# A hybrid decoder layer: from whole-sequence stages in program order to eight interleaved 512-token tiles ordered by a build-time list scheduler

## The chip, the cores and the metric

The kernel runs on all eight cores of one Trainium2 chip. Each core computes two of the sixteen sequences; the cores do not exchange data. The metric is the device time of the slowest core, in microseconds (us). A core has a matrix engine (TensorE, PE in the profile; its weight loads are PEld), a vector engine (VectorE, DVE), a scalar engine (ScalarE, ACT), GpSimd (POOL) and SyncE (SP, which here only issues DMA). Each engine takes its instructions from its own list, in the order in which the program put them there.

The program has a fast and a slow state. In the slow state the cores of one die, or of both, show a lower granted clock and the run takes some per cent longer. Where a median is quoted, it is that of all runs of its kernel, slow ones included; ratios are of fast runs alone.

## The reference

One decoder layer, batch 16, sequence 2048, width 1024. Cut to what matters here:

```python
def swiglu(x, w_gate, w_up, w_down):                 # w: 1024x2816, 1024x2816, 2816x1024
    return (silu(x @ w_gate) * (x @ w_up)) @ w_down

mod = silu(c) @ w_ada + b_ada                        # nine vectors: shift, scale, gate for 3 sub-layers
u = modulate(rmsnorm(h, ffn1_norm), sh1, sc1)
h = h + 0.5 * g1 * swiglu(u, ...)                    # FFN1
u = modulate(rmsnorm(h, mix_norm), sh2, sc2)
h = h + g2 * hybrid_mixer(u, ...)                    # causal attention: 4 differential + 4 latent heads,
                                                     # rope by positions, combined in/out projections
u = modulate(rmsnorm(h, ffn2_norm), sh3, sc3)
h = h + 0.5 * g3 * swiglu(u, ...)                    # FFN2
return rmsnorm(h, final_norm)
```

## The kernel before

The hidden state of a whole sequence (128 x 8 x 2048 fp32) stays in SBUF, and the stages run one after another in program order, for sequence 0 and then for sequence 1. Activations are kept transposed: the width lies on the partitions, so the sum of squares over the width needs a matmul with a matrix of ones.

```python
for s in range(nseq):                                # two sequences per core
    if s > 0:
        load_x(s)
    norm_mod(0, s); ffn(0, s, plans[(s, 0)])         # hooks that spread the adaLN blocks: cut
    norm_mod(1, s); mixer(s, plans[(s, "mix")])
    norm_mod(2, s); ffn(2, s, plans[(s, 1)])
    final_store(s)
```

The norm statistics are squared on ScalarE or VectorE in bf16, and summed by eight matmuls with ones, one for each chunk of 128 of the width:

```python
def stats(srcs, split=True):
    pb = psall.next()                                # one rotation over all eight PSUM banks
    for k, (ap, res) in enumerate(srcs):
        sq, sqR = btmp.next()
        ...                                          # square on DVE or ACT
        I("pe", "matmul", r=[sqR, onesR], w=[PR[pb]], out=PS[pb][:], lhsT=ones_sb[:], rhs=sq[:],
          start=(k == 0), stop=(k == n - 1))
    return pb
```

Weights lie in HBM as fp32. Each use fetches a block through GpSimd's DMA queue, which casts to bf16 on the way, into one of five buffers. A block is used for all 2048 tokens of a sequence before it is released, so a core reads each FFN weight twice in all.

The softmax here doesn't subtract the row's maximum and nothing guards it: scores larger than these inputs give would overflow.

## Time and profile before

Three runs: 3640.93, 3645.35 and 4089.76 us, median 3645.35. The last is slow. (The result below counts a fourth run, 3662.38 us.) In the profiled run all cores lie between 3627.8 and 3640.0 us.

| | before |
|---|---|
| span of the slowest core | 3640.0 us |
| TensorE busy | 3025.7 us, 83% |
| VectorE, ScalarE, GpSimd busy | 50%, 33%, 3% |
| bytes moved by DMA, as counted | 143.53 MB |

The page of the profile, first lines, then three rows of its 40 slices (91 us each): the busy tenths of TensorE, the granted TensorE clock in tenths, and the busy tenths of the DMA engines. Last, a group of VectorE instructions: its line, engine, operation, operands, shape and count, then busy us and the mean ns of one, then the idle time before them.

```profile
span 3640.0 us, 42738 instructions; the slowest of 8 cores (3627.8 to 3640.0 us)
PE 3025.7 (83%) x16784; PEld 1435.4 (39%) x16784; DVE 1828.8 (50%) x3549; ACT 1194.5 (33%) x2001; POOL 98.3 (3%) x121
...
PE   1899996779777769999939999947887777799996
...
PEclk8899998889888879999959999978898887899998
DMA  9243343002001021221361222110010100222112
...
L125 DVE TENSOR_TENSOR ft<-hT,rs 128x512 f32<-128x512 f32 x192 | 117.7, 685 | 133.1 <-ACT rs L125 133.1
```

The nines are the feed-forward networks. The sevens and eights between them (slices 6 to 14 and 26 to 34, counted from 0) are the mixer and its norms. In the same slices the clock row shows mostly 8 and 7: where TensorE has gaps, the granted clock in the records is lower too.

The windows view gives stretches with numbers: the stretch, its length, then busy us (and count) of PE, PEld, DVE, ACT and POOL, the granted clock, the DMA share and GB/s. The four stretches are the start, a norm phase with what is around it, the second half of a mixer, and a feed-forward network.

```profile
0.00:91.00 91.00, 16.26 (x152) 6.04 (x152) 11.76 (x37) 25.23 (x41) 8.97 (x14) 0.85 1.01 184
560.00:700.00 140.00, 88.24 (x454) 37.04 (x453) 106.86 (x197) 65.44 (x109) 5.09 (x6) 0.80 0.21 30
910.00:1365.00 455.00, 328.05 (x2252) 175.44 (x2250) 261.56 (x589) 259.14 (x443) 5.03 (x6) 0.85 0.10 16
1365.00:1820.00 455.00, 452.08 (x2062) 200.07 (x2062) 191.10 (x281) 54.14 (x103) 15.02 (x18) 1.00 0.24 37
```

The last row is dense: 452 of 455 us busy, at clock 1.00. The timeline inside it shows ScalarE's evacuation of one gate bank after every 16 matmuls (eight gate, eight up). Its columns are start, duration, the instruction, and in brackets how long it had waited and for whom:

```profile
1379.59 0.60 ACT L125 ACTIVATE ft<-psall 128x512 f32<-128x512 f32 x1 [2.86 <-PE psall L125]
...
1383.04 0.60 ACT L125 ACTIVATE ft<-psall 128x512 f32<-128x512 f32 x1 [2.86 <-PE psall L125]
```

They come 3.45 us apart, so a matmul of 128x512 takes 3.45 / 16 = 215.6 ns. The Trainium skill, "TensorE: Matmul & The Clock Gate", section "Back-to-back issue gap", gives N / 2.4 + 2.5 ns as the gap of an isolated warm matmul of N columns, 215.8 ns for 512, and says that a sustained stream with weight loads needs only about 131 ns. This trace, a stream with one weight load for each matmul (2062 of each in the last row), agrees with the formula and not with the 131 ns. I use that form below as the **ideal** time of TensorE: each matmul of N columns counts N / 2.4 + 2.5 ns, but one of 129 columns 57 ns (in this trace eight took 0.63 us, and in long runs of them one takes 57 ns) and one of 2 columns 30 ns (a round figure; in this trace they mostly start 25 ns apart). The **lost** time of a stretch is its length less the ideal time of its matmuls. It holds idle time and time at a reduced clock together. For the kernel before, the ideal is 2742 us, and the lost time is 3640 - 2742 = about 900 us: 82 us in the first 91 us, and 334 and 333 us in the two mixers with their norms (560 to 1400 and 2370 to 3200); the rest is spread over norms and seams.

The waits view of TensorE (who was waited for, us in all, times, longest) names what it idles for:

```profile
PE psall L125 <- ACT bt L125: 302.3, 71, 31.0
PE psall L125 <- DVE obf L125: 72.1, 28, 8.5
```

`bt` holds the squares of the norms and the rope inputs, and `obf` is the attention output before its transpose. Neither engine is full; the stages only run one after another.

### The profile page before, as it was taken

How to read it: one execution, taken by the hardware profiler on the slowest of the kernel's cores; microseconds unless marked ns; L12 is line 12 of the kernel's file. 1: busy time of each engine (PE TensorE's matmuls, PEld its weight loads, DVE VectorE, ACT ScalarE, POOL GpSimd, SP SyncE). 2: the span in 40 equal slices, each digit the busy share in tenths (PEclk: the TensorE clock that was granted, in tenths of full speed). 3: DMA queues.
4: the chain of work that ended last, by engine and by line, in shares of the span. 5: the costliest groups of instructions: out<-in, count | busy, mean ns of one | idle time of the engine just before them, and what ended most of it. 6: DMA issues, size and time to landing. Idle time of an engine off the chain costs nothing.

```text
span 3640.0 us, 42738 instructions; the slowest of 8 cores (3627.8 to 3640.0 us)
## 1 busy us (share of the span) xinstructions
PE 3025.7 (83%) x16784; PEld 1435.4 (39%) x16784; DVE 1828.8 (50%) x3549; ACT 1194.5 (33%) x2001; POOL 98.3 (3%) x121
## 2 busy tenths in 40 slices
PE   1899996779777769999939999947887777799996
PEld 0344442344435424444314444424443254344442
DVE  1343447757574462344642334666766645433337
ACT  2301005363636651100152010065454564511112
POOL 0000000000000000000000000000000000000000
PEclk8899998889888879999959999978898887899998
DMA  9243343002001021221361222110010100222112
GB/s 184 44 79 59 58 64 50 15 1 29 1 14 20 13 35 24 42 46 24 52 194 24 35 47 30 24 21 10 15 15 4 29 13 1 35 47 45 26 18 93
DMA packets 123178, 143.53 MB, mean 39 GB/s; under 512 B 5984, under 2 KB 91232, under 8 KB 122976
## 3 DMA queue, kind: packets, MB, share of 16 engines
q0 software_dynamic: 100944, 102.83, 18.6%
q1 hardware_dynamic: 22032, 37.96, 3.6%
q8 instruction: 132, 2.16, 0.2%
q14 instruction: 70, 0.57, 0.1%
HBM read 226.82 MB, written 16.78 MB: 67 GB/s over the span
## 4 chain that ended last, share of the span: by engine, by line
PE 66%; DVE 17%; ACT 10%; issue 3%; DMA 2%; SPq 2%; ACTq 0%; DVEq 0%; POOLq 0%
PE psall L125 66%; DVE hT L125 5%; DVE ft L125 3%; ACT uT L125 3%; DVE accsb L125 3%; ACT ptbuf L125 2%; ACT bt L125 2%; ACT rs L125 2%; SPq L125 2%; DVE small L125 1%; DVE wb L125 1%; DVE bigA L125 1%; DMA hT<-xT 1%; DMA lam_sb<-lamv 1%; DVE junk L125 1%
## 5 line engine op out<-in xcount | busy, mean ns | idle before, releaser
L125 PE MATMUL psall<-uT,wb 128*128 128x512 bf16 (+2 forms) x6688 | 1520.2, 388 | 51.8 <-DVE ft L125 36.9
L125 PEld LDWEIGHTS psall<-uT,wb 128*128 128x128 bf16 (+2 forms) x6688 | 664.1, 100 | 881.0 <-issue 74.7
L125 DVE SCALAR_TENSOR_TENSOR hT<-psall,SC,hT 128x512 f32<-128x512 f32 x960 | 653.3, 744 | 134.1 <-PE psall L125 127.2
L125 ACT ACTIVATE ft<-psall 128x512 f32<-128x512 f32 x352 | 185.6, 601 | 1419.8 <-PE psall L125 1418.2
L125 ACT ACTIVATE ptbuf<-psall 128x512 bf16<-128x512 f32 (+2 forms) x608 | 419.4, 766 | 150.8 <-PE psall L125 146.0
L125 DVE TENSOR_TENSOR bigA<-ft,psall 128x512 bf16<-128x512 f32 x192 | 131.8, 687 | 501.8 <-PE psall L125 483.7
L125 PE MATMUL psall<-bigB,ptbuf 128*128 128x129 bf16 x3264 | 321.3, 233 | 53.4 <-ACT ptbuf L125 27.1
L125 PE MATMUL psall<-bt,ones_sb 128*128 128x512 bf16 x328 | 146.6, 513 | 235.9 <-ACT bt L125 223.5
L125 DVE TENSOR_TENSOR bigB<-ft,psall 128x512 bf16<-128x512 f32 x160 | 109.8, 686 | 455.9 <-PE psall L125 451.7
L125 PE MATMUL psall<-bigA,wb 128*128 128x512 bf16 x1536 | 333.5, 379 | 0.0
L125 PE MATMUL psall<-bigB,wb 128*128 128x512 bf16 x1280 | 292.9, 380 | 4.5
L125 PEld LDWEIGHTS psall<-bigB,ptbuf 128*128 128x128 bf16 x3264 | 223.2, 103 | 147.6 <-ACT ptbuf L125 81.8
L125 PE MATMUL psall<-bigA 64*128 64x512 bf16 (+3 forms) x1216 | 235.7, 334 | 21.8 <-DVE bigA L125 15.6
L125 ACT ACTIVATE bt<-hT 128x512 bf16<-128x512 f32 x256 | 138.3, 616 | 318.9 <-DVE hT L125 160.1
L125 PEld LDWEIGHTS psall<-bigA,wb 128*128 128x128 bf16 x1536 | 150.0, 98 | 180.5
L125 DVE COPY accsb<-psall 128x258 f32<-128x258 f32 x192 | 81.7, 426 | 212.1 <-PE psall L125 208.4
L125 PEld LDWEIGHTS psall<-bigB,wb 128*128 128x128 bf16 x1280 | 117.7, 98 | 176.8 <-DVE hT L125 47.3
L125 DVE TENSOR_TENSOR ft<-hT,rs 128x512 f32<-128x512 f32 x192 | 117.7, 685 | 133.1 <-ACT rs L125 133.1
L125 PEld LDWEIGHTS psall<-bt,ones_sb 128*128 128x128 bf16 x328 | 32.5, 102 | 347.4 <-ACT bt L125 168.5
L125 DVE TENSOR_TENSOR ft<-bigB,psall 128x512 f32<-128x512 bf16 (+1 forms) x208 | 136.5, 682 | 51.5 <-PE psall L125 43.5
L125 PE MATMUL psall<-wb 128*128 128x512 bf16 x512 | 128.2, 405 | 27.4 <-DVE wb L125 18.5
L125 ACT ACTIVATE uT<-ft,SC 128x512 bf16<-128x512 f32 x192 | 138.0, 800 | 19.5 <-DVE ft L125 19.5
(70 smaller groups left out, 1536.3 us busy)
## 6 DMA issues: line engine op xcount, KB each, us to landing
wb<-wg POOLq DMA_DIRECT2D x20, 1024.0 KB, 9.1
wb<-wu POOLq DMA_DIRECT2D x20, 1024.0 KB, 9.6
wb<-wd POOLq DMA_DIRECT2D x20, 1024.0 KB, 9.0
wb<-w_ada POOLq DMA_DIRECT2D x18, 1024.0 KB, 14.8
hT<-xT SPq DMA_DIRECT2D x64, 256.0 KB, 11.9
outT<-hT SPq DMA_DIRECT2D x64, 256.0 KB, 3.6
wb<-w_in POOLq DMA_DIRECT2D x12, 512.0 KB, 5.6
posi<-pos SPq DMA_DIRECT2D x16, 256.0 KB, 3.3
```

Source lines behind the costliest of these rows:

```text
L125: ins = getattr(eng, o.fn[0])(**o.fn[1])
```

## The change

The intent is to give TensorE other work while attention and norms leave gaps. The kernel is rewritten:

- The two sequences are cut into eight tiles of 512 tokens. While attention of tile t runs, FFN2 of tile t-1 and FFN1 of tile t+1 are interleaved with it. K and V of earlier tiles go to HBM and come back.
- Operations are recorded in a graph, each with a cost and a "virtual time" that spreads it over the segment in which it was recorded (`seg(a, b)`). At build time a list scheduler gives each engine, whenever that engine is free, the ready operation of the lowest virtual time. The list is then fixed; on the chip every engine follows it in order.
- Weights are now needed once per tile, not once per sequence. The first use loads fp32 through GpSimd's queue as before, and writes the bf16 block back to HBM; every later use reads the bf16 copy through SyncE's queue.
- The squares of a norm and their sum over the eight chunks move to GpSimd: eight products and seven additions, in a chain, 128x512 each; one matmul with ones is left. Silu is built from tanh.
- The eight PSUM banks are split: 0, 1, 2 rotate for the feed-forward networks (`fb`), 3, 4, 7 for the mixer (`mb`), and attention accumulates in 5 and 6.

The diff is a rewrite of nearly all lines; its core, with cuts marked:

```diff
+fb = Rot([0, 1, 2])                       # PSUM banks of the feed-forward networks, in turn
+mb = Rot([3, 4, 7])
-psall = Rot(list(range(8)))
...
+def load(self, src, scr, key, ...):       # class Ring: weight buffers
+    if key not in self.seen:              # first use: fp32 in, bf16 back to HBM
+        G.dma("pool", ..., out=buf, in_=src)
+        G.dma("sp", ..., out=scr, in_=buf)
+    else:                                 # later uses
+        G.dma("sp", ..., out=buf, in_=scr)
...
+def sumsq(srcs, bank, dim):
+    ...                                   # GpSimd: 8 products, 7 additions -> ar
+    MM(bank, PS[bank], onesf[:], ar[:], True, True, [arR, onesR])
+    ...                                   # ScalarE: Ln, Exp -> rs
...
+for t in range(NT):
+    s1 = 0 if t == 0 else 1
+    base = 2.0 * t if t else 1.0
+    ...                                   # norm for the mixer, spill of h
+    if not last:
+        with G.seg(base + 0.1, base + 0.4, eng="pool"):
+            load_x(t + 1, 1)
+            st1 = hstats(1, fb.next())    # norm statistics of tile t+1: takes a feed-forward bank
+    if t > 0:
+        with G.seg(base, base + 0.667, lead=0.05):
+            gate_up(1)                    # FFN2 of tile t-1: takes feed-forward banks in turn
+    if not last:
+        with G.seg(base + 0.667 if t else 0.9, base + 0.7 if t else 1.0):
+            apply_norm(1, 0, (t + 1) // 4, st1, uF, uFR, ntmp)
+    ...                                   # down(1), final(t-1), gate_up(0) of t+1, projections,
+                                          # attention, out_proj, norm for FFN2, down(0)
```

## The prediction

It was made before any run of the changed kernel, from the profile before, the two programs, and the order of the built program's instructions.

> **What bounds it now.** TensorE, but only in places. In a dense feed-forward stretch (timeline at 1380 us) 16 matmuls of 128x512 take 3.455 us, 215.9 ns each, at a granted clock of 1.00 (windows, 1365:1820). The program has 6.44 million matmul columns; at that rate they need 2714 us (estimate from 215.9 ns per 512). The span is 3640 us. The other 926 us: TensorE idle 614 us (busy 3026), and about 310 us of busy time at a reduced clock. Both sit in the start (0:91 us: TensorE busy 16 us, DMA saturated), the norm phases and the mixer: windows 560:700, 910:1365 and 2730:3185 show TensorE 63 to 74% busy and clock 0.80 to 0.85. The waits view names ACT's norm squares (302 us), rope, attention evacuation and exponentials. VectorE (50%) and ACT (33%) bind only locally: stages run one after another.
>
> **What the change does.** TensorE work hardly shrinks: the built program has 6.23 million columns (mask matmuls and most ones-matmuls gone; norm sums move to GpSimd), estimate 2640 us at 215.9 ns per 512 and 57 ns per 128x129 (eight took 0.63 us in the timeline). The gain is packing: feed-forward matmuls fill the gaps of attention (built order: 4 feed-forward matmuls, 12 PV, 3 QK, ...), so idle and low clock should both vanish in the middle.
> Other engines, counts of the built program times durations here: VectorE about 1450 us (352 gate products at 0.74, 352 up products at 0.69, 208 rope products at 0.68, ...), ACT about 1200 us (736 exponentials at 0.54 to 0.64, 352 tanh at 0.52 to 0.60) plus some 100 table switches at 1.28 us (31 before). Neither reaches 60%.
> Added: weights are reloaded for every 512 tokens from a bf16 copy in HBM, 290 MB, with 150 MB of other traffic and 122 MB of fp32 loads. Before, the first 91 us read about 300 GB/s with DMA full, so some 1.9 ms of DMA, hidden except where fp32 loads, write-back and reloads coincide.
>
> **Sum (estimates).** 2640 TensorE; +60 start before the first feed-forward matmul; +105 in tile 0, whose 34 weight blocks cost 5.2 us each (1 MB fp32 read, 0.5 MB written back) against 3.45 us of matmuls, plus adaLN weights; +20 for the same in the second feed-forward; +55 at the end (last norm, last feed-forward alone, 16 chained GpSimd operations, store); +100 of small waits (static order against true durations, table switches, three PSUM banks per side). Total 2980 us, 18% less. All of the gain lies on the critical path, since TensorE is that path.
>
> **Range and chances.** 2830 to 3190 us. Faster by over 2%: 0.95; within 2%: 0.03; slower: 0.02.
>
> **What the profile would show.** TensorE over 90% busy and clock at least 0.97 from slice 5 to 38; slices 1 to 4 thin, with DMA near full; the chain of waits mostly matmuls, then DMA at the start; ACT table loads near 100.
>
> **What would make it wrong.** (1) The clock. The Trainium skill, "TensorE: Matmul & The Clock Gate", Part 1, says that three or more cores of a die on dense matmuls fall to 13/16. This trace disagrees (1.00 with eight cores dense), but one of three runs took 4090 us, which 13/16 in the dense 1824 us would explain. If denser work brings that state on, about 3400 us. (2) GpSimd's additions and two-input VectorE operations share a port (skill, "SBUF — State Buffer", Who interferes with whom; not shown here): VectorE delays stall the banks. (3) Reload bandwidth when all cores stream. (4) Better packing than I grant: 2800.

Its "about 300 GB/s" is an estimate that counts what the casting loads read, fp32. The windows view counts the bf16 that they write, 184 GB/s; counted the other way, the trace has some 280 GB/s (8.6 MB from casting loads, taken twice, and 8.2 MB from others in 91 us).

## The result

| | before | after |
|---|---|---|
| median of the runs beside each other | 3653.86 us | 3206.95 us |
| all after runs | | 3202.4 to 3207.08 us |
| ratio of fast runs | 1 | 0.8782, 95% interval 0.8747 to 0.8816 |

A ratio here is the mean time of one kernel's fast runs over the mean time of the other's of the same rounds. It is therefore not quite the ratio of the medians quoted. (The median of before in these rounds is pulled up by a slow run.)

The change saves 12%, and the prediction had said 18%: 3207 us against 2980, and outside its range of 2830 to 3190.

The page after, in the same cut (a slice is now 80 us), with two of its VectorE groups, and its line on the chain of waits that ended last:

```profile
span 3204.9 us, 39963 instructions; the slowest of 8 cores (3189.3 to 3204.9 us)
PE 2779.3 (87%) x15704; PEld 1358.9 (42%) x15704; DVE 1382.9 (43%) x2800; ACT 1154.4 (36%) x1996; POOL 693.6 (22%) x670
...
PE   0646789688998999899998999899997999998988
...
PEclk9876789899999999999998999999999999998989
DMA  8999796797554464544435456644754464443123
...
PE 70%; DMA 10%; POOL 7%; DVE 7%; ACT 4%; issue 1%; SPq 1%; POOLq 0%; DVEq 0%; ACTq 0%
...
L303 DVE TENSOR_TENSOR actv<-ft,psall 128x512 bf16<-128x512 f32 x352 | 241.5, 686 | 206.4 <-PE psall L303 205.2
...
L303 DVE TENSOR_TENSOR nt<-h,rs 128x512 f32<-128x512 f32 x128 | 92.5, 743 | 182.2 <-ACT rs L303 174.4
```

The sevens and eights of the mixers are gone. Two things are new. The first ten slices are mostly thin, with DMA at 6 to 9 tenths. And the row of nines is broken by an eight (once a seven) every four or five slices, which is once per tile.

Windows: the start up to the statistics of the first norm, in which TensorE runs only 96 small adaLN matmuls (2 columns each) and one with ones; the rest of the start and tile 0 until just behind its first down-projection, whose last matmul ends at 319 us; the rest of tile 0; tile 1; and tile 3 as one of the steady tiles.

```profile
0.00:75.00 75.00, 3.14 (x97) 2.94 (x97) 2.76 (x18) 2.99 (x4) 29.39 (x37) 1.00 0.83 152
75.00:345.00 270.00, 153.62 (x755) 64.82 (x754) 119.05 (x224) 35.41 (x55) 60.85 (x75) 0.75 0.95 201
345.00:572.00 227.00, 211.70 (x1271) 105.00 (x1272) 120.53 (x285) 88.15 (x147) 60.27 (x70) 0.91 0.83 189
572.00:966.00 394.00, 333.51 (x1776) 159.69 (x1776) 166.34 (x326) 132.01 (x224) 93.62 (x96) 0.94 0.72 186
1333.00:1724.00 391.00, 368.16 (x2253) 189.85 (x2251) 163.19 (x325) 182.10 (x321) 78.08 (x68) 0.98 0.47 142
```

With the lost time computed as before (ideal 2652 us in all, so 553 us lost), set against the terms of the prediction's sum. I read its "+60" and "+105" as the start and tile 0, its "+20" as tile 1, and divide its "+100 of small waits" over what is left:

| stretch | lost, measured | predicted | difference |
|---|---|---|---|
| 0 to 572 us: start and tile 0 | 72 + 149 + 33 = 254 | 60 + 105 = 165 | +89 |
| 572 to 966: tile 1 (first use of the FFN2 weights) | 75 | 20 | +55 |
| 966 to 2775: tiles 2 to 6 | 152 | 100 | +52 |
| 2775 to 3205: last tile and end | 72 | 55 | +17 |
| sum | 553 | 340 | +213 |

Adding the differing ideal (2652 against 2640) gives 225 us, which is the distance from 2980 to the profiled 3205.

TensorE's waits after:

```profile
PE psall L303 <- POOL ar L303: 178.2, 28, 39.3
PE psall L303 <- DMA wf<-w_ada: 41.5, 5, 23.0
PE psall L303 <- DVE ft L303: 34.8, 14, 8.6
PE psall L303 <- DVE cab L303: 32.6, 1, 32.6
```

The first line is the new one. `ar` is the sum of squares that GpSimd hands to the ones-matmul. GpSimd is busy for only 22% of the span, and still TensorE stands for it 178 us. The timeline of a steady tile shows how; `st1`, the statistics of the next tile, is the matmul `psall<-ar,onesf`:

```profile
1741.10 1.04 POOL L303 TENSOR_TENSOR ac<-h 128x512 f32<-128x512 f32 x1 [17.29 <-DMA h<-xT]
...
1745.81 0.61 PE L303 MATMUL psall<-bt,cm 128*128 128x512 bf16 x1 [0.69 <-ACT bt L303]
...
1756.87 1.26 POOL L303 TENSOR_TENSOR ar<-ac,sq 128x512 fp32r<-128x512 f32 x1
...
1758.19 0.80 PE L303 MATMUL psall<-ar,onesf 128*128 128x512 f32 x1 [11.77 <-POOL ar L303]
...
1759.76 3.59 PE L303 MATMUL psall<-uF,wf 128*128 128x512 bf16 x8 [0.78 <-ACT rs L303]
...
1764.77 7.51 PE L303 MATMUL psall<-uF,wf 128*128 128x512 bf16 x34 [1.41 <-DVE ft L303]
```

GpSimd begins when the x of the next tile has landed (1741.10), works through its chain of dependent operations in 17 us, and TensorE stands from 1746.4 to 1758.2. Such a gap comes once in each tile from 1 to 6: 26.7, 12.0, 12.9, 11.8, 12.9 and 12.2 us. (Tile 0 has one of 11.9 us at 341.9 us, which is left out here: taking the bank later, tried below, does not shorten that tile.) The matmuls that follow are `uF,wf`, the gate of FFN2 of the tile before; they need neither `ar` nor `rs`. Why does TensorE not do them first? In the recorded graph `st1` asks for a bank of the rotation `fb` just before `gate_up(1)` does, so a later gate matmul gets the same bank and must wait until `st1`'s result has been read out of it. The graph has that edge, write after write, from the `st1` matmul to the first matmul of the gate that reuses its bank. The order fixed at build time therefore puts `st1`, with virtual time 4.40 in tile 2, in front of gate matmuls of virtual time 4.03. The Trainium skill, "TensorE: Matmul & The Clock Gate", section "Step-by-step: what each phase is for", states that "the MATMULs themselves stay in program order", with only weight loads pulled ahead. This trace agrees in so far as the gate matmuls behind `st1` began only after it, 11.77 us late. It is no separate proof, since these wait for the bank as well: at build time the scheduler found nothing that it could put into the gap.

That is an argument from a trace. Whether the bank is the cause, and what it costs in all, the experiments must show.

### The profile page after: what moved, and what is told of

Read it like the earlier page. It is cut to its first block, busy times and chain, and to the rows that moved or that the text cites. A ratio compares the mean times of both kernels' runs of the same rounds, so it can differ in the third digit from the quotient of the medians.

```text
span 3204.9 us, 39963 instructions; the slowest of 8 cores (3189.3 to 3204.9 us)
## 1 busy us (share of the span) xinstructions
PE 2779.3 (87%) x15704; PEld 1358.9 (42%) x15704; DVE 1382.9 (43%) x2800; ACT 1154.4 (36%) x1996; POOL 693.6 (22%) x670
## 4 chain that ended last, share of the span: by engine, by line
PE 70%; DMA 10%; POOL 7%; DVE 7%; ACT 4%; issue 1%; SPq 1%; POOLq 0%; DVEq 0%; ACTq 0%
PE psall L303 70%; POOL ac L303 3%; POOL sq L303 3%; DVE mt L303 3%; DMA wf<-w_dn 3%; DMA h<-xT 3%; ACT pt L303 2%; DMA s_gu<-wf 2%; DMA wf<-w_gu 1%; POOL ar L303 1%; DVE h L303 1%; SPq L303 1%; DVE lat L303 1%; DMA wf<-s_gu 1%; DMA s_tab<-tab 1%
## 5 line engine op out<-in xcount | busy, mean ns | idle before, releaser
L303 PE MATMUL psall<-uF,wf 128*128 128x512 bf16 x5632 | 1380.9, 387 | 79.3 <-DVE ft L303 34.8
L303 PEld LDWEIGHTS psall<-uF,wf 128*128 128x128 bf16 x5632 | 550.4, 99 | 732.3 <-issue 85.8
L303 PE MATMUL psall<-actv,wf 128*128 128x512 bf16 x2816 | 631.0, 387 | 26.2 <-DMA wf<-w_dn 25.3
L303 ACT ACTIVATE pt<-psall 128x512 bf16<-128x512 f32 (+3 forms) x896 | 440.2, 572 | 79.2 <-PE psall L303 72.1
L303 DVE SCALAR_TENSOR_TENSOR ft<-ft,psall 128x512 f32<-128x512 f32 x352 | 241.1, 686 | 496.0 <-ACT ft L303 496.0
L303 PEld LDWEIGHTS psall<-actv,wf 128*128 128x128 bf16 x2816 | 278.4, 99 | 375.2 <-issue 36.0
L303 DVE TENSOR_TENSOR actv<-ft,psall 128x512 bf16<-128x512 f32 x352 | 241.5, 686 | 206.4 <-PE psall L303 205.2
L303 POOL TENSOR_TENSOR sq<-h 128x512 f32<-128x512 f32 x224 | 233.5, 1050 | 306.6 <-DVE h L303 305.7
L303 POOL TENSOR_TENSOR ac<-ac,sq 128x512 f32<-128x512 f32 x200 | 254.3, 1271 | 11.4
L303 PE MATMUL psall<-uM,wm 128*128 128x512 bf16 x896 | 230.2, 397 | 8.5 <-DMA wm<-s_in 5.3
L303 PEld LDWEIGHTS psall<-pv,pt 128*128 128x128 bf16 x2304 | 159.7, 98 | 76.1 <-ACT pt L303 21.6
## 6 DMA issues: line engine op xcount, KB each, us to landing
wf<-w_gu POOLq DMA_DIRECT2D x44, 512.0 KB, 13.1
s_gu<-wf SPq DMA_DIRECT2D x44, 512.0 KB, 12.9
wf<-w_ada POOLq DMA_DIRECT2D x36, 512.0 KB, 11.2
```

The lines of the kernel that those rows point to most:

```text
L303: ins = getattr(eng, o.fn)(**o.kw)
```

## The experiments

Two questions: what costs about 10 us and more in every tile, and what costs 89 us more than predicted in the start and tile 0?

For the first, theory A says the bank: the dependency is false, and taking `st1`'s bank later removes the gap. Its rivals are a real need (GpSimd's additions as such are too slow, so the wait would only move), and, beside A, an idea A2: a gap costs twice, since the clock falls after it.

For the second, theory B says bandwidth: DMA moves too many bytes at the start, tables and write-backs beside the fp32 weights. The rival is latency: the order in which x, constants and weights arrive.

The ratio is to the fast runs of the kernel before on the same chip. All runs gave correct results. Where the end of a down-projection is given below, it is the end of its last matmul on the core of the profile page. (The expectations say 342 us for the first one of the changed kernel. That is the `st1` matmul after it; the down-projection itself ends at 319 us.) All but the last two ran on one chip.

### e1_control and e1_late_bank: take the bank later

The control splits the statistics into GpSimd's part and TensorE's part and gives `st1` its own fp32 buffer (paid for by one buffer less for squares), without changing when the bank is taken. The other one does the same, and also records the TensorE part after `gate_up(1)`:

```diff
 with G.seg(base + 0.1, base + 0.4, eng="pool"):
     load_x(t + 1, 1)
-    st1 = hstats(1, fb.next())
+    ar1 = sumsq_pool(hsrc(1), arx)                       # GpSimd only, no bank
 if t > 0:
     with G.seg(base, base + 0.667, lead=0.05):
         gate_up(1)
 if not last:
+    with G.seg(base + 0.6 if t else 0.9, base + 0.6 if t else 0.9):
+        st1 = sumsq_fin(ar1, fb.next(), D)               # bank, ones-matmul, Ln, Exp
```

In the control that line reads `st1 = sumsq_fin(sumsq_pool(hsrc(1), arx), fb.next(), D)`.

> The changed kernel with one buffer less for squares and one more for the sum of the next tile's norm, both needed by the next run; its reduction stays in the PSUM bank that it took ahead of the feed-forward. Every theory: 3207 us, within 15 us, and still a gap of about 12 us before the norm reduction in each steady tile. If it moves by more, the next run has to be read against this one.

> The same, but the reduction of the next tile's norm takes its PSUM bank after the gate and up matmuls of the feed-forward have taken theirs. Theory (a false dependency: that reduction was put before the feed-forward in the rotation of three banks, so ready matmuls wait for the load of x and 16 chained GpSimd operations that they do not need): the gap of 12 us goes in six tiles (26 us in the first) and with it the half-clock stretch of 14 to 20 us behind it, which costs half its length: about 20 us per tile, 3207 - 125 = 3080 us (3050 to 3110); TensorE's wait on GpSimd falls from 178 us to under 90. Rival (the load and the GpSimd chain are too slow in themselves): the wait moves to a later place and the time stays within 20 us of the control.

Measured: control 3207.67 us median (fast 3201.79, 3206.77, 3208.57; slow 3362.72), ratio 0.8818 (0.8799 to 0.8837). Late bank 3081.38 us median (fast 3077.34 to 3082.3; slow 3393.48), ratio 0.8468 (0.8455 to 0.8482). The medians differ by 126 us and the means of the fast runs by 125. The edit changes two things, when the bank is taken and the virtual time of `st1` (0.4 becomes 0.6 within the tile). No run separates them, but the builder does, without a chip: with the early bank and the later virtual time it gives TensorE exactly the control's order, and with the late bank and the earlier virtual time exactly that of the late bank. So it is the bank. The builder's own time line also shows the six gaps of the changed kernel, 32.1 us and five times 12.8 us. The control stands where the changed kernel does, so the extra buffer is not what helps.

The window of the tile that answers to the one above, the wait for `ar`, the first and the last instruction of GpSimd's chain, and the window of that chain, all of the late bank:

```profile
1286.00:1656.00 370.00, 364.10 (x2253) 188.99 (x2251) 164.22 (x326) 184.95 (x323) 79.24 (x68) 1.00 0.47 152
```

```profile
PE psall L303 <- POOL ar L303: 85.8, 20, 41.7
```

```profile
1670.29 1.04 POOL L303 TENSOR_TENSOR ac<-h 128x512 f32<-128x512 f32 x1 [14.54 <-DMA h<-xT]
...
1687.18 1.26 POOL L303 TENSOR_TENSOR arx<-ac,sq 128x512 fp32r<-128x512 f32 x1
```

```profile
1670.00:1688.00 18.00, 18.00 (x85) 8.20 (x84) 5.94 (x9) 4.07 (x7) 16.69 (x15) 1.00 0.60 187
```

GpSimd's chain is no shorter (18 us in place of 17), but TensorE is busy in all of these 18 us: the 391 us of the tile became 370 with the same 2253 matmuls, at clock 1.00. The lost time of tiles 2 to 6 fell from 152 to 47 us (8.9, 8.8, 11.2, 9.4, 8.9), and that of tile 1 from 75 to 58. The rival "GpSimd is too slow" falls. What remains of the wait for `ar`, 85.8 us, lies at the start (41.7) and in the other norms, which are real dependencies.

### e2_warm: fill the gap with dummy matmuls

The six gaps add up to 88.5 us, less than the 126 us that the bank cost. Theory A2 says that the rest is the clock after each gap. If so, matmuls that only keep the engine busy in the gap should win the rest. The kernel is the changed one with 64 useless matmuls put in front of `st1`, into its own bank, which is overwritten:

```diff
+bw = fb.next()
+if t > 0:
+    with G.seg(base + 0.39, base + 0.39):
+        for _ in range(64):
+            MM(bw, PS[bw][:, 0:384], ident, ..., True, True, [cmR, HR[1][0]])    # after x has landed
 with G.seg(base + 0.1, base + 0.4, eng="pool"):
-    st1 = hstats(1, fb.next())
+    st1 = hstats(1, bw)
```

> The changed kernel with 64 matmuls of no use (384 columns, into the bank that the norm reduction then overwrites) put where TensorE waits for that reduction, in tiles 1 to 6. The gaps stay as long; only their being idle is taken away. Theory (a gap costs twice, by its length and by the half clock that is granted for 14 to 20 us behind it): half-clock time falls by about 90 us in the trace and the time by about half of that, 3207 - 45 = 3162 us (3145 to 3180). Rival (the clock after a gap costs nothing that matters, other engines set the pace there): 3207 us or more, as 640 us of matmul issue are added in the wrong places.

Measured: 3195.3 us (3190.96 to 3197.12), ratio 0.8782 (0.8768 to 0.8796): 12 us less than the changed kernel, where 45 were expected. In medians of the eight cores 6 of them stand by the end of tile 0, where no dummy matmul was put, and 11 by the end of tile 1; the later tiles are as long as before. The mean clock of the cores rose from 0.940-0.948 to 0.956-0.961, and the time hardly moved. The timeline of e2_warm:

```profile
1736.50 6.50 PE L303 MATMUL psall<-cm 128*128 128x384 bf16 x39
1746.91 0.50 PE L303 MATMUL psall<-ar,onesf 128*128 128x512 f32 x1 [3.91 <-POOL ar L303]
1748.19 3.35 PE L303 MATMUL psall<-uF,wf 128*128 128x512 bf16 x8 [0.78 <-ACT rs L303]
1752.95 7.30 PE L303 MATMUL psall<-uF,wf 128*128 128x512 bf16 x33 [1.41 <-DVE ft L303]
```

The theory that a gap costs twice falls, on the trace of the changed kernel more than on this run. What the profile shows as half clock around a gap covers mostly the gap itself, where no matmul is slowed: the clock records give half clock from 1743.2 to 1763.6 us, and the gap lies from 1746.4 to 1758.2. Eight matmuls behind the gap took 3.59 us in place of 8 x 216 ns = 1.73 us, and the 480 that follow from 1764.77 took 103.6 us, 216 ns each: full speed. The run itself is not a clean test, since a gap of 3.9 us remained and the eight matmuls behind it were still slow (3.35 us). It does show that more clock in the records is not more speed. The rest of the 21 us that a steady tile loses beyond the late bank's is visible in part just behind the gap: the slower `st1` matmul (0.80 us), the wait for `rs` (0.78), 1.86 for the slow eight and 1.41 for the gate's bank, together with the 11.77 some 16.6 us. The last 4 us I did not trace. About as much lies just in front of the gap: waits of 2.17 and 0.69 us, and eight matmuls that took 2.80 us; that gate matmuls would have filled these too is likely, not shown.

### e4_tables: fewer bytes at the start

The changed kernel computes the rope tables of all eight tiles in its start, stores them in HBM (eight stores of 768 KB) and reads them back for each tile. Here the table of tile t+1 is computed in place, right after the projections of tile t have used the last one, and neither stored nor read. That takes the eight stores and seven reads of positions of 256 KB, 8.1 MB, out of the start.

```diff
 with G.seg(-0.1, 0.6, eng="dve"):
     prologue2()
-    for t in range(NT):
-        table(t)
+    table(0)
...
 projections(t)
+if t + 1 < NT:
+    table(t + 1)
 attention(t)
```

> The changed kernel with the sine tables of tiles 1 to 7 made one tile ahead in place, and not all at the start, stored and loaded again: 8 MB less of DMA in the first 345 us, 4 MB less later, two more switches of the ACT table per tile. Theory (the first tile is bound by DMA bandwidth): 8 MB at 200 to 300 GB/s, 25 to 40 us less before the second feed-forward: 3170 to 3185 us. Rival (the start is a chain of latencies, x, norm, adaLN): 3207 us or somewhat more.

Measured: 3173.13 us (fast 3170.07 to 3173.47; slow 3325.63), ratio 0.872 (0.8705 to 0.8736), 34 us less. The end of the first down-projection moved from 319 to 276 us, 43 us earlier (the same in the medians of the cores, 316 to 273), and some of it was given back later. The stretch that ended at 345 us now ends at about 300, in the window of e4_tables:

```profile
79.00:300.00 221.00, 131.70 (x743) 59.75 (x755) 66.16 (x103) 26.19 (x39) 60.49 (x75) 0.85 0.96 197
```

The DMA engines are as full as before (0.96), at the same rate (197 GB/s), and the stretch is shorter by what those bytes take: 8.1 MB at 200 GB/s are 41 us, an estimate from the counted rate. But VectorE also has less to do in this window (66 us against 119), so this run alone doesn't prove bandwidth.

### e3_x_first: the same bytes, x earlier

The x of tile 0 is loaded before everything else, and its statistics are formed while the adaLN weights stream.

```diff
+with G.seg(-1.2, -1.1):
+    load_x(0, 0)
+    ...                                  # two memsets it needs
+    st = hstats(0, fb.next())
 with G.seg(-1.0, -0.9):
     prologue(); ada(1); derive(1); ada(0); derive(0)
-    load_x(0, 0)
 with G.seg(-0.9, -0.8):
-    st = hstats(0, fb.next())
     apply_norm(0, 0, 0, st, uF, uFR, ntmp)
```

> The changed kernel with the first tile's x loaded before the small constants and the adaLN weights, and its sum of squares made at once, instead of after them. TensorE then waits for no GpSimd chain of the first norm (39 us in the profile). Theory (the first tile is bound by the bytes that DMA must move, 90% busy there): the first feed-forward matmul comes 20 to 30 us sooner, but the end of the first feed-forward only 0 to 12 us: 3195 to 3207 us. Rival (the start is a chain of latencies): all of the 25 to 30 us is kept, 3177 to 3182 us.

Measured: 3206.88 us (3196.02 to 3212.45), ratio 0.8799 (0.8769 to 0.8829): no gain. The first 80 us of the changed kernel, and then of this one:

```profile
0.00:80.00 80.00, 4.36 (x129) 3.91 (x129) 5.77 (x25) 5.59 (x7) 31.53 (x41) 1.00 0.84 152
```

```profile
0.00:80.00 80.00, 4.76 (x129) 4.03 (x129) 5.64 (x20) 5.59 (x7) 31.52 (x41) 1.00 0.98 185
```

More bytes came earlier (185 GB/s against 152), and it did not help: the first down-projection ended at 317 us in place of 319. But the step in between failed too. The statistics came 24 us sooner (51.0 us against 74.6), the first feed-forward matmul did not: 93.8 us against 88.6, where 20 to 30 us less were expected. The timeline of e3_x_first shows why:

```profile
84.41 0.43 DVE L303 CAST mt<-mt 128x512 f32<-128x512 int32 x1 [21.59 <-DMA mt<-pos]
...
93.82 1.22 PE L303 MATMUL psall<-uF,wf 128*128 128x512 bf16 x2 [30.41 <-ACT uF L303]
```

In its list VectorE has a cast of the rope positions in front of the last adaLN additions, which `uF`, the normed input, needs, and it stood 21.6 us for these positions. So one link of the chain became shorter and the next one longer. This run shows that x alone is not what the start waits for; it does not decide between bytes and latency.

### e5_bank_tables and e6_bank_tables_x: put together

e5 is e1_late_bank and e4_tables in one; e6 adds e3_x_first.

> The later bank (3081 us) and the tables in place (3173 us) together. They act in different places, the one in tiles 1 to 6 and the other before 345 us, so their gains should add: 3207 - 126 - 34 = 3047 us, within 10 us. If less, one had already hidden the other.

> The last one with the first x loaded first as well. With 8 MB of DMA gone from the start the chain of latencies may matter more: bandwidth theory 3035 to 3047 us; if the start is a chain of latencies, 3015 to 3025 us.

Measured: e5 has two fast runs, 3063.47 and 3064.28 us, and three slow ones (3089.43, 3144.22, 3500.23), so no interval is given. e6 has 3059.35 us median (3053.34 to 3069.97), ratio 0.8401 (0.837 to 0.8432). Both are 12 to 24 us slower than expected. The gains of e1 (126) and e4 (34) add up to 160; from 3207 to 3064 it is 143. The first down-projection ends at 283 us in e5 and at 276 in e4 alone, and against the late bank the tables made in place cost about 2 us in a steady tile. The gain from the earlier x is less than the spread of e6's own runs, and here too the first feed-forward matmul came no sooner (99.0 us, 92.6 in e5), so e6 does not test the chain of latencies either. e6 is the fastest version: 4.6% faster than the changed kernel and 16% faster than the kernel before.

### e7_ffn1_store_later and e8_ffn2_store_later: move bytes, don't remove them

If the start is bound by bytes, then moving the write-back of weights to a later tile should move the lost time with it. In the changed kernel (e7) the FFN1 blocks, and in e6 (e8) the FFN2 blocks, are loaded as fp32 twice, and only the second load is written back:

```diff
 G.dma("pool", ..., out=buf, in_=src)
-if reuse:
+if key[0] in ("gu", "dn") and key[1] == 0 and key not in self.first:    # e8: == 1
+    self.first.add(key); del self.seen[key]                             # no write-back yet
+elif reuse:
     G.dma("sp", ..., out=scr, in_=buf)
```

> The changed kernel, but the bf16 copy of the first feed-forward's weights is written to HBM in the second tile: the first tile loads fp32 and writes nothing, the second loads fp32 again and writes. 17 MB of writes leave the first feed-forward, and its successor in the next tile gets 34 MB more to move. Theory (bandwidth binds the first tile): the first down projection ends 40 to 70 us sooner (342 us before), and all of it or more is given back in the next tile: 3200 to 3260 us in all. Rival (the write-back is hidden and latencies bind): the end moves by less than 10 us.

> The fastest so far (later bank, tables in place, x first; 3055 us), with the bf16 copy of the second feed-forward's weights written in tile 2 instead of tile 1. Tile 1, where DMA is 90% busy for 200 us and TensorE loses 55 us, moves 17 MB less; tile 2, 54% busy, moves 34 MB more. Theory (what is left to lose in tile 1 is bandwidth): 25 to 40 us less in tile 1, at most 10 us more in tile 2: 3020 to 3040 us. Rival (tile 1 loses to something else): 3050 us or more.

Measured, on another chip: e7 3228.02 us (3225.68 to 3229.32), ratio 0.8855 (0.8841 to 0.887). The first down-projection ended at 256 us, 63 us earlier (68 in the medians of the cores), more than e4 won, though VectorE's table work was all still there. The last rows of that down-projection in the changed kernel and in e7, and the window of e7 that answers to e4's (VectorE 130 us busy, where e4 had 66):

```profile
305.94 13.04 PE L303 MATMUL psall<-actv,wf 128*128 128x512 bf16 x44 [4.69 <-DMA wf<-w_dn]
```

```profile
249.52 6.29 PE L303 MATMUL psall<-actv,wf 128*128 128x512 bf16 x28 [0.15 <-DMA wf<-w_dn]
...
79.00:300.00 221.00, 144.68 (x800) 64.97 (x801) 130.33 (x226) 42.71 (x65) 64.91 (x84) 0.85 1.01 184
```

By the end of tile 0 it had been given back, and 21 us more were lost in all. That is what the bandwidth theory expected (40 to 70 us). One rival stays open in e7: a block that is written back also holds its weight buffer until the store has landed (12.9 us, median of `s_gu<-wf`), so the gain could be that of buffers. In e4 no weight buffer is held by the stores that went.

e8 has fast runs of 3060.08, 3064.52 and 3071.05 us (slow 3275.31 and 3411.12), ratio 0.8408 (0.839 to 0.8426): no different from e6, and some 25 to 45 us above what was expected. Windows of e6, then of e8, early in tile 1 and in tile 2:

```profile
533.00:640.00 107.00, 85.03 (x369) 36.20 (x370) 32.32 (x48) 24.36 (x38) 26.89 (x34) 0.94 0.95 221
...
910.00:1262.00 352.00, 345.43 (x2022) 174.23 (x2021) 170.59 (x345) 163.56 (x280) 78.24 (x68) 1.00 0.54 164
```

```profile
533.00:640.00 107.00, 106.34 (x494) 48.06 (x493) 41.95 (x61) 32.91 (x48) 39.43 (x48) 1.00 0.96 168
...
910.00:1262.00 352.00, 306.03 (x1799) 153.25 (x1798) 155.83 (x314) 141.55 (x247) 89.47 (x89) 0.96 0.71 186
```

Early in tile 1 the same 107 us held 494 matmuls in place of 369: the loss there is the write-back's, and the last down-projection of the tile ended at 861 us in place of 903 (in the medians of the cores 35 us earlier). But tile 2, where I had expected room (DMA share 0.54), lost it again: 223 fewer matmuls in its window, and the tile took 400 us in place of 350. I had missed that the fp32 loads come in bursts at the pace of the feed-forward network: a mean share of 0.71 over the tile does not mean that a block comes in time, and TensorE stood 16.5 us for one `w_gu` block, from 916 us on.

The Trainium skill, "DMA: Bandwidth & Descriptors", section "Issuing engines are not separate DMA queues", says that DMA of all issuing engines runs on the same 16 engines and interleaves. e7 and e8 agree: with SyncE's stores gone, the stretch fed by GpSimd's loads ends earlier (63 us in e7, 42 in e8), and where the stores go, the loss goes.

## Why the prediction was wrong

**The ideal of TensorE: right.** 2640 us predicted, 2652 by the rule above from the trace. The gaps of the mixer, some 330 us in each, were indeed filled. The dense stretches were not throttled: they show 1.00, and the mean clock of the slowest core is 0.942.

**The step that failed: "+100 of small waits (static order against true durations, table switches, three PSUM banks per side)".** It named the three banks and treated them as small change. The false dependency that the bank rotation makes cost 126 us by itself (e1_control against e1_late_bank); tiles 2 to 6 lost 152 us, and 47 once the bank was taken later. Without it the kernel takes 3081 us, which is inside the range. It was there to be seen without a run: the built order has `st1` in front of gate matmuls of a lower virtual time, and a wait for GpSimd's chain on it. I had read the built order in a stretch of attention, where the interleaving is as intended, and not where the norm of the next tile begins.

**The term that was mis-sized: "+60 start … +105 in tile 0".** Measured 254 us against 165, of which the bank is no part. The first feed-forward matmul came at 88.6 us, where the sum has 60. I costed the 34 weight blocks (fp32 in, bf16 back) and said "plus adaLN weights" without a number. Left out were 8.1 MB of tables and positions, which cost 43 us of the start and 34 us in all (e4), and beside them x, the mixer's weights and the adaLN blocks that share the same DMA engines. That the stretch behind the first feed-forward matmul is bound by the bytes that DMA moves is what e4 and e7 show together, each with a rival of its own (VectorE's work, held buffers) that the other has not. What the first 89 us wait for stays open: e3 was to test it and did not. How the remaining difference divides over x, adaLN and mixer weights was not measured.

**"+20 for the same in the second feed-forward".** Measured 75 us in tile 1: 17 us of it are the bank's, and most of the rest is the same load and write-back (e8 removed 42 us from the profiled core's tile 1 by moving the write-back). I had assumed that attention of that tile would leave the DMA time to catch up.

**"+55 at the end".** Measured 72 us; it was not examined.

**Clock, point (1) of what could go wrong: did not happen in the dense stretches.** The Trainium skill, "TensorE: Matmul & The Clock Gate", Part 1, says that a die falls to 13/16 of its clock once three of its cores run dense matmuls, and stays there while the load lasts. The fast runs disagree: all eight cores of e6 run at mean clocks of 0.967 to 0.972. In a slow run of e5 four cores of one die ran at 0.807 to 0.812 and took 3482 to 3499 us, and the other die ran the same program at 0.966 to 0.970 and took at most 3063 us. So a state near 13/16 exists here, but denser work did not bring it on in every run, and no run shows what does. It also comes in pieces: in the profiled fast run of the changed kernel the clock records of cores 2 and 3, the latter the one on the page, hold 81 and 74 us at 0.8125, all between 209 and 373 us, a stretch that is not dense (TensorE busy for 89 of 163 us; window 252:272: clock 0.81). The other six cores have none, nor has any core of the control, which takes as long, so these pieces don't explain the result.

**GpSimd and VectorE, point (2): present, and small.** The skill, "SBUF — State Buffer", section "Who interferes with whom", says that a VectorE instruction with two SBUF inputs contends with a GpSimd instruction that reads SBUF, and one with a single SBUF input does not. The traces agree. The norm's product of two SBUF tiles took 685 ns before and 743 after (`ft<-hT,rs`, `nt<-h,rs`), while `actv<-ft,psall`, with one input in PSUM, stayed at 686 (687 before, as `bigA<-ft,psall`). Over all such groups, worked out from counts and means, that is about 25 us of VectorE's 1383, and VectorE is not what binds.

**What I said the profile would show.** "TensorE over 90% busy and clock at least 0.97 from slice 5 to 38" failed, first in slices 5 to 9, which were DMA's, and then once in each tile, which was the bank's. "Slices 1 to 4 thin with DMA near full" held, and went on up to slice 9. ScalarE's table loads were 90, near the 100 that I gave.

## What to carry to other kernels

When a scheduler orders a program by dependencies, a buffer or bank taken early by a slow chain is a dependency too: take the bank where its first write is due, not where the chain begins, and look through the built order for an instruction that stands in front of others whose virtual time is earlier. In a list that is followed in order such an edge can cost most of the latency of the slow chain (here some 12 of 17 us in each tile), although the engine of that chain is mostly idle. And when weights are read more often so that stages can overlap, add up every byte of the first pass, tables and write-backs with it: there is no computation yet to hide it, and bytes that are only put off are paid for in the next tile.

## What the Trainium skill lacked or had wrong

- "TensorE: Matmul & The Clock Gate", Part 1, gives the 13/16 clock as what follows from three dense cores of a die. Here eight dense cores ran at mean clocks of 0.967 to 0.972 in e6's fast runs, and the same kind of program fell to 0.807 to 0.812 on one die in a slow run of e5. It is a state of some runs here; and in a fast run two cores of a die alone had 0.8125 for 81 and 74 us, in a stretch that was not dense.
- The same page says how long matmuls stay slow after an idle time, but not that the half-clock time in the records lies mostly over the gap itself. One record of 20.4 us at half clock holds a gap of 11.8 us; behind that gap eight matmuls took 3.59 us in place of 1.73, and the next 480 took 216 ns each. Read as a cost, the record misled me into e2.
- "SBUF — State Buffer", Who interferes with whom, says who blocks whom but not how much a mixed program feels. Here, with chains of 15 instructions on GpSimd beside VectorE, the mean of the norm's product of two SBUF tiles rose from 685 to 743 ns.
- "DMA: Bandwidth & Descriptors" has no figure for fp32 loads cast to bf16 with a write-back beside them on all eight cores at once. Here, at a DMA share of 0.95, 201 GB/s were counted, and a block of 512 KB (bf16) landed in 13.1 us (median of the `w_gu` loads) where a plain bf16 reload took 4.3 us.
- None of the pages that I read tells what a false dependency through a PSUM bank costs. Here it was 126 us of 3207.
